# Channel mixer of a decoder layer: gate and up by seven block products over two pairs of chunks, the down projection summed in PSUM in a phase of its own

## The chip, the cores and the metric

The kernel runs on one core of a Trainium2 chip. The metric is the device time of one launch in microseconds (us), median of three runs; the trace is of one more, profiled execution. Engines are called as in the profile: PE (TensorE matmuls), PEld (its weight loads), DVE (VectorE), ACT (ScalarE), POOL (GpSimd), SP (the queue that issues most DMAs).

## The reference, cut to what matters

One layer: a token mixer (RWKV-7, mLSTM, sliding-window and forgetting attention, then an output projection) and a channel mixer. Only the second is changed:

```
D_MODEL, SEQ, D_FF = 1024, 2048, 2816                       # float32
h = _rmsnorm(x, norm_ffn_pre)
gate, up = jnp.split(h @ ffn_w_up, 2, axis=-1)               # 2048x1024 @ 1024x5632
gate = _causal_dwconv(gate, ffn_conv_w, ffn_conv_b)          # width 3, along the sequence
f = jax.nn.gelu(gate, approximate=True) * up
x = x + _rmsnorm(f @ ffn_w_down, norm_ffn_post)              # 2048x2816 @ 2816x1024
```

## The kernel before

Each float32 operand of a large product is scaled by a power of two and split into two float16 parts, high and low. One product of two numbers is then three float16 matmuls: high x high, high x low, low x high. The 2048 tokens are four chunks of 512 (`C`), each four tiles of 128 (`P`); the 2816 channels are 22 blocks of 128 (`NF`).

`stage2` ends with the output projection. `o_tiles(c)` works on the four token tiles of chunk c: load of y, split, two DMA transposes into `yt` (one buffer), 96 matmuls of 128x256, norm, add to x, a second norm (`norm_u`, with two `rsqrt`, each a `pow` on POOL), two DMA transposes into the operand `U2[c]` (`V` in the profile). `o_tiles(2)` and `o_tiles(3)` come last.

`stage_n`, lines 1463 to 1552, is the channel mixer. A loop over 11 groups `g` of two channel blocks loads and splits the group's weights: `split_w` loads pieces of 128x1024 through the stage tile `wst`, takes the maximum on DVE (L233), reduces it over the partitions with `partition_all_reduce` on POOL (L238), makes the power of two by three tiny DVE operations (`pow2`, L204 to L206), writes the high part on ACT (L252) and the low one on DVE (L253). Then for each chunk and block: `gemm_cm` (L265 to L267), 24 matmuls of 128x512 into `psg` for the gate and 24 into `psu` for up; ACT copies the gate to `gb` (L1504), DVE makes the convolution (L1508 to L1510), ACT the GELU (L1511), DVE the product with `psu` (L1515) and its maximum (L1516). After both blocks a `partition_all_reduce` (L1519) gives the scale, ACT and DVE split f (L1526, L1527), and for each token tile and half of the outputs six matmuls (L1535 to L1537) make a partial sum in `psd` that DVE adds to the accumulator `acc` in SBUF (L1541). The last group ends with norm, residual and store (L1543 to L1552). All 16 `acc` tiles live in SBUF.

A planner (the tile framework with a timeline simulation) puts the instructions of each engine in a fixed order; on the chip each engine takes them in that order, so a waiting instruction holds up all behind it on its engine.

Of the kernel before, what the change touches and what calls it, by code (L numbers as in the profile page):

```python
# [97 lines left out]
def _layout(inp):  # L98
# [19 lines left out]
    up = a["ffn_w_up"].reshape(KT, P, 2, NF, P).transpose(3, 1, 0, 2, 4)  # L118
# [21 lines left out]
class Trunk:  # L140
# [14 lines left out]
    def setup(self):  # L155
# [19 lines left out]
        for n, k in enumerate(("g1", "g2")):  # L175
# [6 lines left out]
            nc.vector.tensor_scalar(out=self.ug[:, n:n + 1], in0=un, scalar1=2.0 ** -9, scalar2=None, op0=ALU.mult)  # L182
# [17 lines left out]
    def pow2(self, m, e):  # L200

        nc = self.nc
        o = self.small.tile([P, 3], F32, name="p2")
        nc.vector.tensor_scalar(out=o[:, 0:1], in0=m, scalar1=1e-30, scalar2=2.0 ** -e, op0=ALU.max, op1=ALU.mult)  # L204
        nc.vector.tensor_scalar(out=o[:, 1:2].bitcast(I32), in0=o[:, 0:1].bitcast(I32), scalar1=0x7F800000, scalar2=None, op0=ALU.bitwise_and)
        nc.vector.reciprocal(out=o[:, 2:3], in_=o[:, 1:2])  # L206
        return o[:, 1:2], o[:, 2:3]
# [83 lines left out]
    def norm_u(self, pool, x, n, grow, U, i, h=None, bufs=1):  # L291
# [6 lines left out]
        self.rsqrt(ss[:, 1:2], ss[:, 0:1], 2.0 ** -18 / D, 2.0 ** -18 * EPS)  # L298
# [563 lines left out]
    def stage2(self):  # L862
        with ExitStack() as ck, ExitStack() as co:
# [597 lines left out]


    def stage_n(self):
        nc = self.nc
        GF = 2
        NG = NF // GF
        with ExitStack() as ctx:
            small = self.pool(ctx, "small_n", bufs=4)
            sw = self.pool(ctx, "small_nw", bufs=2)
            self.wp = self.pool(ctx, "w_n", bufs=1)  # L1470
            self.stage = self.pool(ctx, "st_n", bufs=2)
            wk = self.pool(ctx, "wk_n", bufs=2)
# [112 lines left out]
```

## Time and profile before

| | us |
|---|---|
| median of 3 runs | 3137.87 (3135.27 to 3146.45) |
| the profiled execution | 3138.18 |
| its span, first to last instruction | 3136.0 |
| output projection over (last matmul on `Wo`) | about 1753 |
| last matmul of the channel mixer | about 3117.6 |

A row of a group of instructions has the line, the engine, the operation, output <- inputs, shape and count, then busy time, mean ns of one, and the idle time of the engine before it with what ended it. A matmul's row overlaps the next one's, so the pace is read from starts or from counts in a window. Times in a timeline are us from the start of the span.

### The profile page before, as it was taken

The numbers are of one execution on the slowest core, as the hardware profiler recorded it, in microseconds if no ns is written. First come the engines' busy times: TensorE is split into PE (matmuls) and PEld (weight loads), VectorE is DVE, ScalarE is ACT, GpSimd is POOL, SyncE is SP. The second block draws the span as 40 slices with busy tenths as digits, with TensorE's granted clock in tenths as the row PEclk, the third lists the DMA queues.
The fourth block names the chain that finished last, engine by engine and source line by source line (L and its number), as shares of the span: only waits on it lengthen the run. The fifth ranks groups of instructions, "written<-read, shape, count | busy, mean of one in ns | idle before, by whom it ended". The sixth has DMA issues, their size and how long they took to land. (4 is left out here: it accounts for less than half of the span.)

```text
span 3136.0 us, 46311 instructions
## 1 busy us (share of the span) xinstructions
PE 2840.9 (91%) x17902; PEld 1697.3 (54%) x17902; DVE 1893.1 (60%) x4159; ACT 942.1 (30%) x1812; POOL 599.5 (19%) x957
## 2 busy tenths in 40 slices
PE   1599889999989998799987899999999999999995
PEld 0145577777767776577764444444444444444442
DVE  3464565568776554577765565655656656556565
ACT  2342232345452224366652221111211211212121
POOL 1243222223324332132221100000000000000033
PEclk9799899998988999799998899999999999999998
DMA  6442323345652365565544210000100100001023
GB/s 177 101 111 60 91 68 101 88 107 137 153 138 77 86 184 150 142 151 140 125 109 108 61 41 14 27 27 14 41 14 28 41 14 27 28 14 41 14 101 114
DMA packets 322396, 256.08 MB, mean 82 GB/s; under 512 B 215488, under 2 KB 269120, under 8 KB 322176
## 3 DMA queue, kind: packets, MB, share of 16 engines
q1 hardware_dynamic: 252320, 200.67, 23.6%
q10 hardware_dynamic: 69856, 52.46, 6.0%
q8 instruction: 140, 2.29, 0.3%
q14 instruction: 80, 0.66, 0.1%
HBM read 153.26 MB, written 66.49 MB: 70 GB/s over the span
## 5 line engine op out<-in xcount | busy, mean ns | idle before, releaser
L1541 DVE SCALAR_TENSOR_TENSOR acc<-psd,uns,acc 128x512 f32<-128x512 f32 x320 | 237.1, 750 | 209.2 <-PE psd L1537 207.9
L1535 PE MATMUL psd<-hi_dn,fh 128*128 128x512 f16 x704 | 269.8, 383 | 18.2 <-ACT fh L1526 18.1
L267 PE MATMUL psg<-V,lo_up 128*128 128x512 f16 x704 | 268.8, 382 | 9.4 <-DVE lo_up L253 9.4
L1536 PE MATMUL psd<-lo_dn,fh 128*128 128x512 f16 x704 | 269.5, 383 | 0.0
L265 PE MATMUL psg<-V,hi_up 128*128 128x512 f16 x704 | 268.7, 382 | 0.0
L266 PE MATMUL psg<-V,hi_up 128*128 128x512 f16 x704 | 268.7, 382 | 0.0
L267 PE MATMUL psu<-V,lo_up 128*128 128x512 f16 x704 | 267.4, 380 | 0.0
L266 PE MATMUL psu<-V,hi_up 128*128 128x512 f16 x704 | 267.1, 379 | 0.0
L265 PE MATMUL psu<-V,hi_up 128*128 128x512 f16 x704 | 267.1, 379 | 0.0
L1537 PE MATMUL psd<-hi_dn,fl 128*128 128x512 f16 x704 | 262.4, 382 | 1.8 <-DVE fl L1527 1.8
L267 PEld LDWEIGHTS <-lo_up 128*128 128x128 f16 x1408 | 138.1, 98 | 176.4 <-DVE lo_up L253 9.9
L265 PEld LDWEIGHTS <-hi_up 128*128 128x128 f16 x1408 | 138.0, 98 | 166.5 <-issue 1.7
L266 PEld LDWEIGHTS <-hi_up 128*128 128x128 f16 x1408 | 138.0, 98 | 166.5 <-issue 1.4
L275 PE MATMUL psg<-Wo,yt 128*128 128x256 f16 x512 | 144.7, 284 | 42.8 <-DMA yt<-hl 42.7
L1504 ACT ACTIVATE gb<-psg,un_up 128x512 f32<-128x512 f32 x88 | 60.2, 684 | 386.4 <-PE psg L267 386.4
L265 PE MATMUL psg<-U,hi_cm 128*128 128x512 f16 x256 | 103.9, 406 | 69.7 <-ACT hi_cm L252 69.7
L1506 POOL COPY gtail<-gb 128x2 f32<-128x2 f32 x88 | 19.8, 225 | 768.6 <-ACT gb L1504 768.6
L233 DVE TENSOR_REDUCE wm<-wst 128x1 f32<-128x1024 f32 (+1 forms) x91 | 109.7, 1206 | 88.5 <-DMA wst<-in_w_up 50.7
L265 PE MATMUL psf<-U,hi_fm 128*128 128x256 f16 x576 | 162.3, 282 | 0.0
L267 PE MATMUL psf<-U,lo_fm 128*128 128x256 f16 x576 | 162.2, 282 | 0.0
L266 PE MATMUL psf<-U,hi_fm 128*128 128x256 f16 x576 | 162.1, 281 | 0.0
L277 PE MATMUL psg<-Wo,yt 128*128 128x256 f16 x512 | 141.6, 281 | 5.2 <-DMA yt<-hl 5.2
(428 smaller groups left out, 6400.7 us busy)
## 6 DMA issues: line engine op xcount, KB each, us to landing
wst<-in_w_up SPq DMA_DIRECT2D x44, 512.0 KB
wst<-in_w_dn SPq DMA_DIRECT2D x22, 512.0 KB
zin<-zR SPq DMA_DIRECT2D x80, 128.0 KB
ka<-kA ACTq DMA_DIRECT2D x40, 256.0 KB
wst<-in_w_cm SPq DMA_DIRECT2D x17, 512.0 KB
zR<-m SPq DMA_DIRECT2D x32, 256.0 KB
wso<-in_w_o SPq DMA_DIRECT2D x32, 256.0 KB
xr<-in_x ACTq DMA_DIRECT2D x16, 512.0 KB
```

The costliest lines, as they stand in the source:

```text
L233: nc.vector.tensor_reduce(out=m[:, i:i + 1], in_=st[:, :w], axis=AX.X, op=ALU.max, apply_absolute_value=True)
L265: nc.tensor.matmul(ps[:, sl], lhsT=hi[:, k, n0:n0 + nn], rhs=uh[:, k, sl], start=k == 0, stop=False)
L266: nc.tensor.matmul(ps[:, sl], lhsT=hi[:, k, n0:n0 + nn], rhs=ul[:, k, sl], start=False, stop=False)
L267: nc.tensor.matmul(ps[:, sl], lhsT=lo[:, k, n0:n0 + nn], rhs=uh[:, k, sl], start=False, stop=k == KT - 1)
L275: nc.tensor.matmul(ps, lhsT=uh[:, k, sl], rhs=hi[:, k, n0:n0 + nn], start=k == 0, stop=False)
L277: nc.tensor.matmul(ps, lhsT=ul[:, k, sl], rhs=hi[:, k, n0:n0 + nn], start=False, stop=k == KT - 1)
L1504: nc.scalar.activation(out=gb[:, 2:], in_=pg, func=AF.Copy, scale=un)
L1506: nc.gpsimd.tensor_copy(out=prev[jj], in_=gb[:, C:C + 2])
L1535: nc.tensor.matmul(ps, lhsT=fh[:, jj, sl], rhs=dh[:, o], start=jj == 0, stop=False)
L1536: nc.tensor.matmul(ps, lhsT=fh[:, jj, sl], rhs=dl[:, o], start=False, stop=False)
L1537: nc.tensor.matmul(ps, lhsT=fl[:, jj, sl], rhs=dh[:, o], start=False, stop=jj == GF - 1)
L1541: nc.vector.scalar_tensor_tensor(out=acc[t][:, ns], in0=ps, scalar=uns, in1=acc[t][:, ns], op0=ALU.mult, op1=ALU.add)
```

## The change

The channel mixer becomes two phases.

First phase. The chunks form two pairs. For one channel block and one pair, gate and up of both chunks are a 2x2 block product: weights (gate, up) x (lower, upper half of the 1024 inputs) times activations (halves of the inputs) x (two chunks). It is made by seven block products instead of eight, with three sums of weight blocks (`S`) and four of activations (`T`, made once per pair by `combine`). The products are accumulated in part in three PSUM tiles a, b, c (two buffers each): a product is added to a bank that ACT or DVE has read before. The 22 blocks are taken one at a time; `up_weights` loads and prepares the next block's weights, forms `S` with four POOL operations and takes the maximum of the down weights; `ffn_up` makes the products, the convolution, GELU and product over both chunks at once, stores f as float32 to DRAM (`fD`) and notes its maximum. `f_scale` makes one scale per chunk at the end.

Second phase. `ffn_down` loads the down weights again (split once, kept in SBUF) and f from DRAM, splits f and sums all 22 blocks in PSUM: for chunk 0 in eight banks with the block as the outer loop, for chunks 1 to 3 tile by tile. Then scale, norm, residual and store. The accumulator in SBUF is gone.

The diff, cut to its core (the layout of `w_up`, the vector form of `pow2` and two scale exponents are left out):

```diff
@@ stage2
                     if c <= 2:
                         self.o_tiles(c - 1)
             ck.close()
-            u2b = self.pool(self.ctx, "u2b")
+            keep = self.pool(self.ctx, "keep_n")
...
+            u2b = self.pool(self.cb, "u2b")
             for c in range(2, NC):
                 self.U2[c] = u2b.tile([P, 2, KT, C], F16, name=f"V{c}")
+            self.Tc = [u2b.tile([P, 4, 2, 4, C], F16, name="T0")]
+            self.tails = {}
             for c in range(2, NC):
                 self.o_tiles(c)
+                if c == 2:
+                    self.combine(0, lambda n: self.ow.tile([P, 4, W], F32, name="xs"), self.Tc[0])
+    def combine(self, p, buf, T):
...
+        for k in range(4):
+            for t in range(0, C, W):
...
+                for n, o in enumerate((0, 2, 1, 3)):
+                    nc.gpsimd.tensor_tensor(out=x[:, o], in0=B[n][:, 0, k, ts], in1=B[n][:, 1, k, ts], op=ALU.add)
+                for o, a, b in ((0, 1, 0), (1, 3, 1), (3, 3, 0), (2, 2, 3)):
+                    nc.vector.tensor_tensor(out=x[:, o], in0=x[:, a], in1=x[:, b], op=ALU.subtract)
+                nc.scalar.copy(out=T[:, :, 0, k, ts], in_=x)
+                nc.vector.tensor_tensor(out=T[:, :, 1, k, ts], in0=x, in1=T[:, :, 0, k, ts], op=ALU.subtract)
@@ stage_n
+            W = {j: self.up_weights(j) for j in range(2)}
...
+            for j in range(2):
+                self.ffn_up(0, j, W[j])
+            self.combine(1, ...)
+            for j in range(2):
+                self.ffn_up(1, j, W.pop(j))
+            for j in range(2, NF):
...
+                if j + 1 < NF:
+                    W[j + 1] = self.up_weights(j + 1)
+                w = W.pop(j)
+                for p in range(2):
+                    self.ffn_up(p, j, w)
+                    if j == NF - 1:
+                        self.f_scale(p)
...
+        self.ffn_down()
+    def up_weights(self, j):
+        W = self.wp.tile([P, 2, 7, C], F16, name="Wup")             # two buffers
+        R = self.raw.tile([P, 4, C], F32, name="raw", tag="raw")    # one buffer
+        nc.sync.dma_start(out=R.rearrange("p s n -> p (s n)"), in_=self.A["w_up"][j])
...
+        nc.vector.tensor_reduce(out=m[:, 0:1], in_=R..., op=ALU.max, apply_absolute_value=True)
+        nc.gpsimd.partition_all_reduce(m[:, 1:2], m[:, 0:1], P, RMAX)
+        un, sc = self.pow2(m[:, 1:2], 12)
+        nc.vector.tensor_tensor(out=m[:, 2:3], in0=un, in1=self.ug[:, 1:2], op=ALU.mult)
+        S = self.raw.tile([P, 3, C], F32, name="S")
+        gt = lambda o, x, y, op: nc.gpsimd.tensor_tensor(out=o, in0=x, in1=y, op=op)
+        gt(S[:, 1], R[:, 2], R[:, 0], ALU.subtract)
+        gt(R[:, 0], R[:, 0], R[:, 1], ALU.add)
+        gt(S[:, 0], R[:, 0], R[:, 2], ALU.subtract)
+        gt(S[:, 2], R[:, 3], S[:, 0], ALU.subtract)
+        for o, x in ((slice(0, 4), R), (slice(4, 7), S)):
+            nc.scalar.activation(out=W[:, 0, o], in_=x, func=AF.Copy, scale=sc)
+            nc.vector.scalar_tensor_tensor(out=W[:, 1, o], in0=x, scalar=sc, in1=W[:, 0, o], ...)
+        nc.sync.dma_start(out=d, in_=self.A["w_dn"][j])
+        nc.vector.tensor_reduce(out=self.mD[:, j:j + 1], in_=d, ...)
+    def ffn_up(self, p, j, w):
...
+        product(a, 2, "B11", True)          # 12 matmuls of 128x512 each
+        nc.scalar.activation(out=X, in_=a, func=AF.Copy, scale=un)
+        product(b, 4, "T2", True)
+        add(g2, b, X)                       # DVE: out = b * un + X
+        product(a, 3, "B21", False)         # added to what stands in a
+        nc.scalar.activation(out=gb[:, 2:C + 2], in_=a, func=AF.Copy, scale=un)
+        product(b, 5, "T3", False)
+        add(up[:, 1], b, X)
+        product(c, 0, "T1", True)
+        add(up[:, 1], c, up[:, 1])
+        product(b, 1, "T4", False)
+        add(up[:, 0], b, X)
+        product(c, 6, "B22", False)
+        add(g2, c, g2)
...
+        nc.scalar.activation(out=t, in_=gb[:, 2:], func=AF.Identity, scale=fw(2), bias=...)      # 128x1024
+        nc.vector.scalar_tensor_tensor(out=t, in0=gb[:, 1:2 * C + 1], scalar=fw(1), in1=t, ...)
+        nc.vector.scalar_tensor_tensor(out=t, in0=gb[:, 0:2 * C], scalar=fw(0), in1=t, ...)
+        nc.scalar.activation(out=t, in_=t, func=AF.Gelu_apprx_tanh)
+        nc.gpsimd.tensor_tensor(out=t, in0=t, in1=up..., op=ALU.mult)
+        nc.sync.dma_start(out=self.fD[j][:, p * 2 * C:(p + 1) * 2 * C], in_=t)
+        nc.vector.tensor_reduce(out=self.mF[:, 2 * p:2 * p + 2, j:j + 1], in_=F, ...)
+    def ffn_down(self):
...
+            for j in range(NF):
+                weights(j)                  # ACT queue: load 512 KB (three buffers); ACT high part, DVE low part
+                f = values(0, j)            # SP queue: load 256 KB (four buffers); ACT high part, DVE low part
+                for i in range(NSUB):
+                    for n in range(2):
+                        mms(ps[i][n], f, i, n, j)               # 3 matmuls of 128x512
+                    if j == NF - 1:
+                        out(0, i, ps[i])
+            for c in range(1, NC):
+                F = [values(c, j) for j in range(NF)]           # 30 buffers for f in all
+                for i in range(NSUB):
+                    ps = [bank() for n in range(2)]
+                    for j in range(NF):
+                        for n in range(2):
+                            mms(ps[n], F[j], i, n, j)
+                    out(c, i, ps)
```

## Rows read from the trace of the kernel before

**Rows 1.** The page: the line of PE's busy share, the granted clock in 40 slices of the span, and what the DMA engines moved in each.

```profile
PE 2840.9 (91%) x17902; PEld 1697.3 (54%) x17902; DVE 1893.1 (60%) x4159; ACT 942.1 (30%) x1812; POOL 599.5 (19%) x957
...
PEclk9799899998988999799998899999999999999998
...
GB/s 177 101 111 60 91 68 101 88 107 137 153 138 77 86 184 150 142 151 140 125 109 108 61 41 14 27 27 14 41 14 28 41 14 27 28 14 41 14 101 114
```

**Rows 2.** Busy time of each engine by stretch of the span: end of the output projection, the channel mixer up to its last chunk, 200 us of its middle, and three stretches at the end. Columns: from:to, length, busy us (and count) of PE, PEld, DVE, ACT, POOL, granted clock, DMA share, GB/s.

```profile
1633.60:1753.10 119.50, 81.72 (x525) 54.16 (x524) 58.51 (x99) 35.79 (x57) 20.80 (x23) 0.83 0.44 115
1753.10:3092.80 1339.70, 1331.18 (x6147) 599.84 (x6144) 807.46 (x1347) 245.97 (x340) 108.36 (x265) 1.00 0.10 33
2000.00:2200.00 200.00, 200.00 (x928) 90.24 (x926) 117.25 (x199) 33.05 (x46) 9.41 (x35) 1.00 0.06 19
3092.80:3104.00 11.20, 0.00 (x0) 0.00 (x0) 4.46 (x9) 1.29 (x3) 1.42 (x2) 0.62 0.51 161
3104.00:3117.60 13.60, 13.21 (x48) 5.24 (x48) 7.49 (x13) 4.13 (x8) 2.34 (x3) 0.81 0.00 0
3117.60:3136.00 18.40, 0.00 (x0) 0.00 (x0) 6.53 (x7) 1.15 (x2) 10.09 (x6) 0.64 0.46 171
```

**Rows 3.** The first stretch of rows 2 again, only the matmuls that read the operand V of the channel mixer: length, PE busy and count, clock, DMA share, GB/s.

```profile
1633.60:1753.10 119.50, 35.77 (x141) 0.83 0.44 115
```

**Rows 4.** Groups of DVE instructions by line, between 2000 and 2400 us (busy, mean ns, idle before).

```profile
L1541 DVE SCALAR_TENSOR_TENSOR acc<-psd,uns,acc 128x512 f32<-128x512 f32 x104 | 77.0, 750 | 66.3 <-PE psd L1537 66.0
L233 DVE TENSOR_REDUCE wm<-wst 128x1 f32<-128x1024 f32 x20 | 24.4, 1220 | 25.9 <-DMA wst<-in_w_up 16.7 <-DMA wst<-in_w_dn 9.2
...
L1510 DVE SCALAR_TENSOR_TENSOR gc<-gb,pc,gc 128x512 f32<-128x512 f32 x26 | 19.5, 751 | 0.6
...
L253 DVE SCALAR_TENSOR_TENSOR lo_up<-wst,p,hi_up 128x1024 f16<-128x1024 f32 x12 | 15.1, 1280 | 1.5 <-ACT hi_up L252 1.5
```

**Rows 5.** The same view and stretch for ACT.

```profile
L1504 ACT ACTIVATE gb<-psg,un_up 128x512 f32<-128x512 f32 x25 | 17.1, 685 | 128.8 <-PE psg L267 128.8
...
L252 ACT ACTIVATE hi_up<-wst,p 128x1024 f16<-128x1024 f32 x12 | 13.1, 1141 | 35.4 <-PE psu L266 35.1
```

**Rows 6.** The same view for POOL, the whole span.

```profile
L1551 POOL TENSOR_TENSOR wst<-wst,acc 128x1024 f32<-128x1024 f32 x16 | 39.5, 2471 | 18.2 <-DMA wst<-x2buf 7.8 <-DVE acc L1550 6.5 <-DVE rsq L214 4.0
L427 POOL TENSOR_TENSOR m<-z 128x512 f32<-128x512 f32 x32 | 35.2, 1100 | 22.0 <-issue 22.0
```

**Rows 7.** POOL's timeline in the token mixer and the output projection: start, length, line, operation; in brackets the idle time before and what ended it ("issue": nothing that the profile shows).

```profile
88.93 1.03 POOL L427 TENSOR_TENSOR m<-z 128x512 f32<-128x512 f32 x1 [7.19 <-issue]
...
102.56 0.38 POOL L238 PARTITION_ALL_REDUCE wmm<-wm  x1 [5.90 <-issue]
...
380.69 0.71 POOL L534 TENSOR_TENSOR bon<-bon,r_ln_b 128x256 f32<-128x256 f32 x1 [7.08 <-issue]
...
1674.00 0.38 POOL L238 PARTITION_ALL_REDUCE wmm<-wm  x1 [11.72 <-DVE rsq L214]
```

**Rows 8.** DVE's timeline at two of those places.

```profile
90.00 0.75 DVE L428 SCALAR_TENSOR_TENSOR m<-m,pc,z 128x512 f32<-128x512 f32 x1 [7.04 <-POOL m L427]
90.66 0.15 DVE L205 TENSOR_SCALAR p<-p 128x1 int32<-128x1 int32 x1
...
1650.55 0.15 DVE L204 TENSOR_SCALAR p<-wmm 128x1 f32<-128x1 f32 x1 [6.19 <-POOL wmm L238]
1650.62 0.74 DVE L1509 SCALAR_TENSOR_TENSOR gc<-gb,pc,gc 128x512 f32<-128x512 f32 x1
```

**Rows 9.** PE's timeline behind the second of them.

```profile
1655.07 0.38 PE L266 MATMUL psg<-V,hi_up 128*128 128x512 f16 x1
1664.85 0.61 PE L267 MATMUL psg<-V,lo_up 128*128 128x512 f16 x1 [9.41 <-DVE lo_up L253]
1665.25 0.64 PE L265 MATMUL psg<-V,hi_up 128*128 128x512 f16 x1
1665.68 0.63 PE L266 MATMUL psg<-V,hi_up 128*128 128x512 f16 x1
```

**Rows 10.** The timeline of DVE and POOL near the end: two DVE operations, each beside a POOL operation of 128x1024.

```profile
3091.50 2.34 POOL L1551 TENSOR_TENSOR wst<-wst,acc 128x1024 f32<-128x1024 f32 x1
3091.53 2.86 DVE L1509 SCALAR_TENSOR_TENSOR gc<-gb,pc,gc 128x512 f32<-128x512 f32 x1
...
3120.76 0.73 DVE L1541 SCALAR_TENSOR_TENSOR acc<-psd,uns,acc 128x512 f32<-128x512 f32 x1
3120.85 2.34 POOL L1551 TENSOR_TENSOR wst<-wst,acc 128x1024 f32<-128x1024 f32 x1 [1.16 <-DVE rsq L214]
```

**Rows 11.** The output projection's timeline: the last matmul of one token tile and the first of the next that waited, the transposes between them, and the transposes of the very last tile into V.

```profile
1632.80 0.27 PE L277 MATMUL psg<-Wo,yt 128*128 128x256 f16 x1
1641.13 0.28 PE L277 MATMUL psg<-Wo,yt 128*128 128x256 f16 x1 [0.81 <-DMA yt<-hl]
```

**Rows 12.** SP's DMA issues there.

```profile
1748.40 18.93 SPq L289 DMA_TRANSPOSE V<-hl  x4
```

**Rows 13.** The end of the timeline: the restart of PE after its idle stretch, the last square and the last stores.

```profile
3104.12 0.61 PE L1535 MATMUL psd<-hi_dn,fh 128*128 128x512 f16 x1 [11.41 <-ACT fh L1526]
...
3121.61 1.06 ACT L1548 ACTIVATE njunk<-acc 128x1024 bf16<-128x1024 f32 x1 [4.62 <-DVE acc L1541]
...
3130.21 2.63 SPq L1552 DMA_DIRECT2D out<-wst  x2
```

More of the change, by code (lines that the diff above doesn't have):

```diff
@@ L202, in pow2 @@
         nc = self.nc
[L203 to L207, printed above, removed]
+        n = m.shape[-1]
+        o = self.small.tile([P, 3 * n], F32, name=f"p2_{n}")
+        nc.vector.tensor_scalar(out=o[:, 0:n], in0=m, scalar1=1e-30, scalar2=2.0 ** -e, op0=ALU.max, op1=ALU.mult)
+        nc.vector.tensor_scalar(out=o[:, n:2 * n].bitcast(I32), in0=o[:, 0:n].bitcast(I32), scalar1=0x7F800000, scalar2=None, op0=ALU.bitwise_and)
+        nc.vector.reciprocal(out=o[:, 2 * n:3 * n], in_=o[:, n:2 * n])
+        return o[:, n:2 * n], o[:, 2 * n:3 * n]
     def rsqrt(self, out, v, mul, eps):
@@ new lines, in stage_n @@
+            self.sn = self.small = self.pool(ctx, "small_n", bufs=4)
+            self.raw = self.pool(ctx, "raw_n", bufs=1)
+            self.wp = self.pool(ctx, "w_n", bufs=2)
+            self.wk = self.pool(ctx, "wk_n", bufs=2)
+            self.psw = self.pool(ctx, "ps_w", bufs=2, space=PSUM)
+            tp = self.pool(ctx, "t1_n", side="right")
+            W = {j: self.up_weights(j) for j in range(2)}
+            self.Tc.append(tp.tile([P, 4, 2, 4, C], F16, name="T1"))
+            for j in range(2):
+                self.ffn_up(0, j, W[j])
@@ new lines, in f_scale @@
+    def f_scale(self, p):
+        nc, small = self.nc, self.sn
+        self.small = small
+        if p == 0:
+            md = small.tile([P, 2], F32, name="md", bufs=1)
+            nc.vector.tensor_reduce(out=md[:, 0:1], in_=self.mD, axis=AX.X, op=ALU.max)
+            nc.gpsimd.partition_all_reduce(md[:, 1:2], md[:, 0:1], P, RMAX)
+            un, sc = self.pow2(md[:, 1:2], 14)
+            nc.vector.tensor_copy(out=self.sd[:, 0:1], in_=un)
+            nc.vector.tensor_copy(out=self.sd[:, 1:2], in_=sc)
+        mm = small.tile([P, 4], F32, name="mm")
+        nc.vector.tensor_reduce(out=mm[:, 0:2], in_=self.mF[:, 2 * p:2 * p + 2], axis=AX.X, op=ALU.max)
+        nc.gpsimd.partition_all_reduce(mm[:, 2:4], mm[:, 0:2], P, RMAX)
+        un, sc = self.pow2(mm[:, 2:4], 14)
+        nc.vector.tensor_scalar(out=self.sf[:, 2 * p:2 * p + 2, 0], in0=un, scalar1=self.sd[:, 0:1], scalar2=None, op0=ALU.mult)
+        nc.vector.tensor_copy(out=self.sf[:, 2 * p:2 * p + 2, 1], in_=sc)
@@ L1554, in run @@
     def run(self):
-        self.cu, self.cr_, self.cf = ExitStack(), ExitStack(), ExitStack()
+        self.cu, self.cr_, self.cf, self.c2, self.cb = (ExitStack() for n in range(5))
         self.setup()
@@ L1561, in run @@
         if "N" in self.phases:
-            if "2" not in self.phases:
-                self.u2p = self.pool(self.ctx, "u2")
-                self.U2 = [self.u2p.tile([P, 2, KT, C], F16, name=f"V{c}") for c in range(NC)]
-                for c in range(NC):
-                    self.nc.sync.dma_start(out=self.U2[c], in_=self.pre_u[c])
             self.stage_n()
```

196 lines of the change are left out of this document (106 added, 90 removed).

## The prediction

> **What bounds the kernel now.** I read the page first: PE is busy 91% of the span, with the clock at its upper level in the second half [rows 1]. A busy share is no rate, so the windows come next. In the middle of the channel mixer PE starts 928 matmuls of 128x512 in 200 us, one every 0.2155 us, without a gap, while DVE is busy 59% and DMA idle [rows 2]. So this stage is bound by the number of matmuls. From 1753.1 to 3092.8 us stand 6147 of them; at that pace they take 1324.7 of 1339.7 us, so 15.0 are lost. Behind come 11.2 us without PE (the last chunk's scale), 48 matmuls in 13.6 us instead of 10.3, and a tail of 18.4 us [rows 2]. The reader should see a front end too: before 1753.1 the mixer had already run 141 matmuls in holes of the output projection [rows 3], worth 30.4 us. So the mixer stands as if it had begun at 1722.7 and run without filler: 1413.3 us = 6336 x 0.2155 (1365.4) + 47.9 lost.
>
> **The change, part by part.**
>
> Matmuls. Gate and up took 22 blocks x 4 chunks x 48 = 4224; seven products of 12 for 2 pairs make 22 x 2 x 84 = 3696. The down projection keeps 22 x 4 x 4 x 2 x 3 = 2112. So 528 fewer, 113.8 us at the pace of [rows 2]: 3696 take 796.5 us (36.2 per block), 2112 take 455.1.
>
> Removed beside PE: 320 additions into acc, 750 ns each [rows 4], about 240 us of DVE, and the scales per chunk. They stood beside matmuls and are worth nothing by themselves.
>
> Load per block in the first phase, by the durations of [rows 4 to 6]. DVE: ten additions out of PSUM 7.5 us, four convolution steps of 128x1024 at 1.28, maxima of f 2.4, of the weights 2.4 and 1.2, low parts of 128x2048 and 128x1536 by the slope from 0.75 (512) to 1.28 (1024) 2.3 + 1.8, small ones 0.6: 23.3 of 36.2 us, or 64%, against 59% now. ACT: four evacuations 2.7, and some 8 for the wide operations at 1.14 for 1024 columns: 30%. POOL: two products 4.9, four sums at 1.1, an all-reduce 0.4: 9.7. No engine but PE is full; the matmul bound stays, if the waits allow.
>
> The waits are the point. In-place accumulation makes PE wait for an engine inside a unit (one block, one pair): a's second product needs ACT's read of the first, and three products on b and c need DVE's read of what stands there. Each read is due while one other product runs, 12 x 0.2155 = 2.59 us; result latency, read (0.75) and signal take some 1.1, so DVE may be 1.5 us late and no more. Queued behind a DVE instruction that waits are just these reads, and behind them PE.
>
> And DVE will wait, for POOL. On POOL each change between the all-reduce and a TENSOR_TENSOR costs a pause that no instruction explains: 5.90 us into the reduce, 7.08 and 7.19 back out of it; one reduce whose pause fell into waiting time started at once [rows 7], so the pause counts from POOL's previous instruction. The planner doesn't foresee it: DVE stood 7.04 us at a waiting operation with a ready one (L205) behind it, and 6.19 us in the same way at L204 [rows 8], after which PE idled 9.41 us [rows 9]. In the middle of the mixer now POOL runs only reduces and copies, so it never changes. The new phase changes twice per block. Placed as the program has it: subtraction (1.1), all-reduce, three sums (3.3). The reduce is due about 2.6 us after the weights land and comes at 1.1 + 5.9 = 7.0: DVE's `pow2` stands B = 4.4 us. POOL then is through 17.8 us after landing (7.0 + 0.4 + 7.1 + 3.3), while the product of a unit falls due at about 12: it is 5.8 us late, less what PE lost before, and DVE stands some 4.3 us again at the maximum of f. Of a stand of B, 1.5 us are slack and DVE's spare 36% of the mean way to the next urgent read (3.9 us, from their distances 5.2, 2.6 and 10.3) returns 1.4. So PE loses 1.5 us the first time, and about 1.0 the second, when POOL has partly caught up: 2.5 per block, 55 us in all. Bounds: 0, if the reduces fall into POOL's idle time, and both pauses less slack, (5.9 - 1.5) + (7.1 - 1.5) = 10.0 per block, 220 us. I take 55 as each way in part is covered by POOL's spare 26 us per block.
>
> The port. A DVE operation with two SBUF inputs took 2.86 us beside a POOL operation of 2.34, one that reads PSUM and SBUF its usual 0.73 [rows 10]. The Trainium skill (SBUF — State Buffer, Who interferes with whom) says the same: only two SBUF inputs, or the two-port modes, contend with GpSimd. By it the new reads out of PSUM stay free, and six two-input operations per block meet 9.3 us of POOL work that was not there; taking the rows' delays for an estimate, 1 to 2 us of DVE per block, inside the slack. Without the rule, by the rows alone, the sum is the same: nothing added, at most 22 x 1.4 = 31 us.
>
> The front. The last four token tiles took 119.5 us [rows 2]. Without matmuls of the mixer between them the chain is 96 matmuls of 256 columns, at half of 0.2155 each 10.3 us, plus 8.3 from the last one to the next tile's [rows 11], about 19 to 20: over at 1633.6 + 78 = 1712. The first pair's `combine` (32 POOL sums, 24 us of DVE) and two all-reduces with four pauses stand on the same queues: I put the end at 1730, between 1712 and 1753. The first unit's work tiles probably share memory with the projection's (40 KB of weights and 28 of work tiles beside some 170 of operands and new pools, by the shapes in the code), free when the last transposes land, 1767.3 [rows 12], 14 us after the last matmul. Three of seven products (7.8 us) fit ahead of that: 7 lost (0 to 14). The second `combine` starts then too, takes some 40 us of DVE beside the units' own work and is covered by two units (36.2): 10 lost (0 to 25). So the mixer stands as if begun at 1747 instead of 1722.7: 24 us worse, between 11 better and 70 worse.
>
> The turn between phases. f of chunk 0 needs the first pair's scale, whose chain runs beside the last unit (18.1 us); first weights and values can be split before. 5 us, between 0 and 20 (today's like gap took 11.2 [rows 13]).
>
> The second phase. Chunk 0 takes in 768 KB per block of 5.17 us, 152 GB/s, and the next chunk's values beside it; the profile shows 171 GB/s at a DMA share of 0.46 [rows 2] and 184 in a slice [rows 1]. 5 us, between 0 and 25. Chunks 1 to 3 need a 256 KB value per 1.29 us only for a quarter of their time, with 30 buffers: 2. The DRAM round trip writes 1 MB per block in the first phase beside 1.5 MB of loads: 69 GB/s, hidden. Tail: last sum, square 1.06 and its chain, one store [rows 13]: 10.5 us by adding 0.9, 1.3, 0.3, 0.8, 1.4, 1.3 and some 4.5 for the store.
>
> Sum: 1747 + 3696 and 2112 matmuls 1251.6 + 55 + 5 + 5 + 2 + 10.5 = 3076 for the span. The profiled run took 2.2 more than its span (3138.18), and stands 0.3 above the median: 3078, 60 us or 1.9% faster.
>
> **The rivals.**
>
> A. The pauses are hidden: POOL idles 26 us of 36.2 per block. Then 55 us less: 3023.
>
> B. POOL holds up DVE in full, place: `pow2` behind the reduce and the maximum of f behind the product. 220 instead of 55: 3243. It speaks for it that [rows 8, 9] show just this, and that reads are more urgent here. It decides the sign where a block loses over (3138 - 3023) / 22 = 5.2 us.
>
> C. The clock. Lost time of 1 to 3 us comes in every unit. Rows: after 9.41 us of idling, matmuls start 0.425 us apart, the lower level, 1.2 GHz [rows 9]; in the dense middle the granted clock is 1.00 [rows 2]. If a fifth of the first phase falls to the lower level, 0.2 x 796.5 = 159 more: 3237. The Trainium skill (TensorE: Matmul & The Clock Gate, A second HAM failure mode: psum-queue depth-cycling) warns of this: PE pausing briefly between groups of matmuls as banks are cycled can swing the clock between its levels. No row here shows it for pauses under 5 us.
>
> D. The change doesn't give a second phase that PE bounds: chunk 0 is fed at the 101 GB/s of an early slice [rows 1]. 22 x 0.786 MB take 171 us instead of 114: 3135, no change.
>
> **How the numbers follow.** A measurement of this kernel can tell some 0.5%, 16 us, from no change. My forecast 3078 with its own range 3040 to 3125: 0.55, of which 0.50 is faster and 0.05 same. A: 0.17, faster. B: 0.18, of which 0.15 is slower and 0.03 same, since a partial loss between forecast and B is as likely as B itself. C: 0.05, slower. D: 0.05, same. Together 0.67 faster, 0.13 same, 0.20 slower. The range goes from a little under A, 3015, to 3180, the half of B that lies next to the forecast; what is left out is a front end at its best with A, and the rest of B and C.
>
> **What would show it.** Right: 36 to 41 us per block in the first phase, DVE idle before `pow2` and before the maximum of f with POOL as releaser, POOL pauses of 6 to 7 us twice per block, granted clock near 1.00. A: windows with a start every 0.2155 us. B: PE idle over 5 us per block, released by DVE. C: a granted clock under 0.95 from 1770 to 2600. The front: the last matmul on `Wo` near 1730. The turn: PE idle under 10 us where `fD` is first read. Wrong altogether if a queue that I counted as hidden (ACT behind its DMA issues, SP behind the store of f) shows up as PE's releaser.

## The result and the profile after

The changed kernel takes 3190.69 us (median; 3186.59 to 3195.55), the kernel before on the same chip 3142.16: a ratio of 1.0146, 95% interval 1.0099 to 1.0193. It is 1.5% slower; forecast was 1.9% faster, and 3190.69 lies above the range's 3180. The profiled run took 3187.6, its span is 3185.6 us, 109.6 over the 3076 of the sum. Matmul counts are as forecast. One run of e12_sums_vector below took 8700.25 us; its median and ratio go by the other three.

The page of the changed kernel, the lines that answer to [rows 1]: busy time, granted clock by slice, GB/s by slice.

```profile
PE 2780.7 (87%) x17374; PEld 1665.5 (52%) x17374; DVE 1707.7 (54%) x3515; ACT 1043.6 (33%) x1844; POOL 808.4 (25%) x990
PEclk9799889899989998899987789999999999999999
GB/s 177 102 109 58 92 66 104 91 95 147 150 134 65 109 167 167 128 139 133 122 90 126 94 125 53 53 53 44 54 49 53 53 53 40 290 107 87 66 73 20
```

PE is less busy than before (91%). Its windows by stage, against [rows 2]: length, then busy time and count of PE, PEld, DVE, ACT, POOL, granted clock, DMA share, GB/s. The stages are the first 200 us of the first phase, its rest, the turn, the second phase, the tail.

```profile
1751.20:1951.20 200.00, 148.79 (x604) 62.66 (x605) 125.44 (x139) 46.57 (x43) 60.99 (x64) 0.85 0.29 98
1951.20:2692.30 741.10, 695.57 (x3093) 308.49 (x3091) 386.94 (x423) 190.87 (x182) 192.30 (x178) 0.97 0.13 50
2692.30:2717.80 25.50, 0.00 (x0) 0.10 (x1) 6.80 (x16) 4.17 (x5) 3.07 (x3) 0.57 0.40 132
2717.80:3176.30 458.50, 458.45 (x2112) 207.21 (x2111) 125.05 (x154) 109.80 (x154) 44.66 (x30) 0.99 0.31 105
3176.30:3185.60 9.30, 0.11 (x1) 0.00 (x0) 3.41 (x4) 1.40 (x3) 0.55 (x1) 0.72 0.14 56
```

Read them by the pace of [rows 2], 0.2155 us a matmul. What a stretch takes beyond its count at that pace is called its loss from here on. 604 matmuls are worth 130.2 us: the start loses 69.8. 3093 are worth 666.5: the rest loses 74.6, though its PE looks 94% busy: 45.5 us stand idle (741.10 - 695.57), and the other 29.1 are matmuls slower than the pace. The turn stands 25.5 us without a matmul. The second phase is dense: 458.5 for 455.1.

Where the 74.6 go shows in one block. The timeline of POOL, DVE and PE (start, length, engine, line; in brackets the idle time before and its releaser):

```profile
2150.98 1.27 POOL L1537 TENSOR_TENSOR S<-raw 128x512 f32<-128x512 f32 x1 [16.39 <-DVE up L1568]
2152.21 2.35 POOL L1602 TENSOR_TENSOR F<-F,up 128x1024 f32<-128x1024 f32 x1
2160.82 0.38 POOL L1533 PARTITION_ALL_REDUCE wm<-wm  x1 [6.25 <-issue]
2168.45 1.44 POOL L1537 TENSOR_TENSOR raw<-raw 128x512 f32<-128x512 f32 x1 [7.25 <-issue]
...
2154.59 1.22 DVE L1604 TENSOR_REDUCE mF<-F 128x2 f32<-128x1024 f32 x1 [0.77 <-POOL F L1602]
2161.22 0.15 DVE L205 TENSOR_SCALAR p<-wm 128x1 f32<-128x1 f32 x1 [5.41 <-POOL wm L1533]
...
2161.74 0.74 DVE L1568 SCALAR_TENSOR_TENSOR up<-psb,wm,X 128x512 f32<-128x512 f32 x1
...
2157.19 2.75 PE L1565 MATMUL psc<-V,Wup 128*128 128x512 f16 x12
2162.54 4.44 PE L1565 MATMUL psb<-T,Wup 128*128 128x512 f16 x12 [2.60 <-DVE up L1568]
2166.81 2.75 PE L1565 MATMUL psa<-V,Wup 128*128 128x512 f16 x12
```

POOL ends the product f at 2154.56, pauses 6.25 us without a releaser, runs the all-reduce, pauses 7.25 us again. DVE stands 5.41 us at `pow2` (L205). The addition behind it (L1568, a read that PE waits for) starts at 2161.74, and PE idles 2.60 us. Then twelve matmuls take 4.44 us instead of 2.75: the clock has fallen to its lower level. One block loses 2.6 + 1.7 = 4.3 us.

The waits between 1960 and 2560 us, some 15 blocks (who waited for whom: us in all, times, longest):

```profile
DVE p L205 <- POOL wm L1533: 75.1, 14, 5.7
DVE mF L1604 <- POOL F L1602: 50.9, 29, 4.1
...
PE psb L1565 <- DVE up L1568: 39.1, 15, 2.9
```

So DVE stands 5.4 + 3.5 us a block behind POOL, and PE idles 2.6. These are all the waits of PE in the rest (its groups by form; the three other groups, `psa` and `psc`, have none):

```profile
L1565 PE MATMUL psb<-T,Wup 128*128 128x512 f16 x1332 | 329.5, 401 | 45.5 <-DVE up L1568 45.5
```

The start has one thing more, the reductions for the maximum of the down weights (tile view: count, durations, first and last start; below, what their engine waited for):

```profile
L1548 DVE TENSOR_REDUCE mD<-rd x22: 1203/1210/1220, 1757.7 to 1916.2; 128x1 f32<-128x1024 f32 x22
...
  DMA rd<-in_w_dn: 10.5, 6
```

All 22, meant one a block, were drawn into the first 165 us. They depend on nothing but a load. The last matmul on `Wo` (same view) answers to the 1730 of the forecast:

```profile
L276 PE MATMUL psg<-Wo,yt x512: 272/273/437, 1288.7 to 1736.4; 128*128 128x256 f16 x171
```

The turn, timeline of DVE, ACT with its DMA issues, and PE:

```profile
2697.75 0.16 DVE L1622 COPY sf<-p 128x2 f32<-128x2 f32 x1
...
2712.78 0.17 DVE L1622 COPY sf<-p 128x2 f32<-128x2 f32 x1
...
2713.03 1.31 ACTq L1638 DMA_DIRECT2D wdr<-in_w_dn  x3
...
2714.87 0.72 ACT L1649 ACTIVATE f<-fr,sf 128x512 f16<-128x512 f32 x1 [11.90 <-issue]
2716.65 1.15 ACT L1642 ACTIVATE Wd<-wdr,sd 128x1024 f16<-128x1024 f32 x1 [1.05 <-DMA wdr<-in_w_dn]
...
2717.85 42.43 PE L1656 MATMUL psd<-Wd,f 128*128 128x512 f16 x184 [25.59 <-ACT Wd L1642]
```

Chunk 0's scale is there at 2697.75. Its weights are asked for at 2713.03, after the second pair's scale.

### The profile page after: what moved, and what is told of

Same layout as the page of the kernel before. It is cut to its first block, busy times and chain, and to the rows that moved or that the text cites. A ratio compares the mean times of both kernels' runs of the same rounds, so it can differ in the third digit from the quotient of the medians.

```text
span 3185.6 us, 45085 instructions
## 1 busy us (share of the span) xinstructions
PE 2780.7 (87%) x17374; PEld 1665.5 (52%) x17374; DVE 1707.7 (54%) x3515; ACT 1043.6 (33%) x1844; POOL 808.4 (25%) x990
## 4 chain that ended last, share of the span: by engine, by line
PE 44%; issue 11%; DVE 10%; DMA 9%; POOL 4%; ACT 3%; SPq 0%; ACTq 0%; POOLq 0%; DVEq 0%
PE psd L1656 10%; PE psb L1565 6%; PE psc L1565 3%; PE psa L1565 3%; DMA raw<-in_w_up 3%; DVE Wup L1544 2%; POOL F L1602 2%; PE psf L268 1%; PE pso L1338 1%; PE psf L266 1%; PE psf L267 1%; DMA yt<-hl 1%; DMA y<-ybuf 1%; PE psf L276 1%; PE psf L278 1%
## 5 line engine op out<-in xcount | busy, mean ns | idle before, releaser
L1565 PEld LDWEIGHTS <-Wup 128*128 128x128 f16 x3696 | 371.2, 100 | 584.0 <-issue 148.2
L1656 PE MATMUL psd<-Wd,f 128*128 128x512 f16 x2112 | 458.6, 380 | 25.6 <-ACT Wd L1642 25.6
L1565 PE MATMUL psb<-T,Wup 128*128 128x512 f16 x1584 | 400.3, 406 | 84.9 <-DVE up L1568 64.2
L1656 PEld LDWEIGHTS <-f 128*128 128x128 f16 x2112 | 207.3, 98 | 276.8 <-ACT f L1649 23.9
L1565 PE MATMUL psa<-V,Wup 128*128 128x512 f16 x1056 | 252.1, 385 | 25.0 <-ACT Wup L1543 21.8
L276 PE MATMUL psg<-Wo,yt 128*128 128x256 f16 x512 | 148.4, 290 | 49.8 <-DMA yt<-hl 41.6
L278 PE MATMUL psg<-Wo,yt 128*128 128x256 f16 x512 | 144.5, 287 | 6.2 <-DMA yt<-hl 6.2
L277 PE MATMUL psg<-Wo,yt 128*128 128x256 f16 x512 | 148.1, 290 | 0.0
L276 PE MATMUL psf<-hi_fv,U 128*128 128x256 f16 (+1 forms) x512 | 139.1, 278 | 2.0 <-ACT zc L779 2.0
L277 PE MATMUL psf<-lo_fv,U 128*128 128x256 f16 (+1 forms) x512 | 139.1, 277 | 0.0
L278 PE MATMUL psf<-hi_fv,U 128*128 128x256 f16 (+1 forms) x512 | 139.0, 277 | 0.0
L268 PE MATMUL psg<-U,lo_cm 128*128 128x512 f16 x256 | 103.2, 404 | 33.1 <-DVE lo_cm L254 19.0
L1328 ACT ACTIVATE fP<-psf,ln2k 128x512 f32<-128x512 f32 (+3 forms) x160 | 98.2, 624 | 98.6 <-PE psf L1324 41.8
L1568 DVE SCALAR_TENSOR_TENSOR up<-psb,wm,X 128x512 f32<-128x512 f32 x88 | 65.8, 747 | 110.5 <-PE psb L1565 110.3
```

The costliest lines, as they stand in the source:

```text
L268: nc.tensor.matmul(ps[:, sl], lhsT=lo[:, k, n0:n0 + nn], rhs=uh[:, k, sl], start=False, stop=k == KT - 1)
L276: nc.tensor.matmul(ps, lhsT=uh[:, k, sl], rhs=hi[:, k, n0:n0 + nn], start=k == 0, stop=False)
L277: nc.tensor.matmul(ps, lhsT=uh[:, k, sl], rhs=lo[:, k, n0:n0 + nn], start=False, stop=False)
L278: nc.tensor.matmul(ps, lhsT=ul[:, k, sl], rhs=hi[:, k, n0:n0 + nn], start=False, stop=k == KT - 1)
L1328: nc.scalar.activation(out=e[:, o:], in_=ps[:, o:], func=AF.Exp, scale=-1.0, bias=self.ln2k)
L1565: nc.tensor.matmul(ps, lhsT=W[:, a, n, ks], rhs=rhs[u](b, k), start=first and k == 0 and i == 0, stop=k == 3 and i == 2, skip_group_check= ...
```

## The experiments

Theory: GpSimd's pauses around the all-reduce make VectorE, which works in order, stand at `pow2` and at the maximum of f; PE waits for the reads queued behind it, and its clock adds to that. Rivals: VectorE is too slow for the folds; the port that GpSimd shares with it; the two phases as such. Times are medians, ratios against the kernel before on the same chip. All stage lengths are of single profiled executions. The runs stand on two chips, and a difference of a few us between two of them says nothing by itself. The code ahead of the mixer is the same in most runs and yet ends its attention anywhere from 1620 to 1658 us, so stages are compared by length and loss, not by place.

**Who makes PE wait**

```diff
 # e1_vector_sums
-gt = lambda o, x, y, op: nc.gpsimd.tensor_tensor(...)
+gt = lambda o, x, y, op: nc.vector.tensor_tensor(...)
-nc.gpsimd.tensor_tensor(out=t, in0=t, in1=up, op=mult)
+nc.vector.tensor_tensor(out=t, in0=t, in1=up, op=mult)
```

> The four weight sums of a block and its two products f go from GpSimd to VectorE, so that GpSimd keeps the all-reduces, the small copies and the memsets and no longer pauses between two kinds of programs inside a block. Theory (VectorE stands in order behind the all-reduce, 5.4 us a block, because GpSimd pauses 6 to 7 us on each side of it; TensorE loses 2.6 us of waiting a block and 1.7 us more at the lower clock after it): the 74.5 us lost between 1950 and 2692 us fall under 25, the time falls by 45 to 75 us. Rival (VectorE itself is too slow a reader of the products): VectorE gets 4 x 0.75 + 2 x 1.28 = 5.6 us more work a block, the loss grows, and the time rises by 20 to 100 us.

3068.12 us, ratio 0.9749 (0.9716 to 0.9782): 123 us under the changed kernel. Windows of its first phase, first 200 us and rest:

```profile
1759.60:1959.60 200.00, 177.30 (x768) 77.07 (x769) 161.43 (x188) 57.08 (x53) 30.02 (x45) 0.94 0.31 109
1959.60:2593.90 634.30, 632.59 (x2930) 286.40 (x2928) 439.74 (x506) 180.34 (x172) 20.13 (x70) 1.00 0.15 55
```

2930 x 0.2155 = 631.4 of 634.3: a loss of 2.9 instead of 74.6, with VectorE busy 69% instead of 52%. The start loses 34.5 instead of 69.8, the turn 17.0 instead of 25.5; I had counted on the rest alone, so the time fell by more than I expected. VectorE is not too slow.

```diff
 # e2_no_reduce
-nc.gpsimd.partition_all_reduce(m[:, 1:2], m[:, 0:1], P, RMAX)
+nc.vector.tensor_copy(out=m[:, 1:2], in_=m[:, 0:1])
```

> The all-reduce of each weight block's maximum is left out: every partition uses its own maximum (one copy on VectorE), so the powers of two differ between partitions. The sums and the products stay on GpSimd. Theory (pauses around the all-reduce, and VectorE's wait behind it): the loss between 1950 and 2692 us falls from 74.5 to under 20, the time by 50 to 75 us. Rival (the port: GpSimd's sums and products slow VectorE and hold it off): they all remain, and the time stays within 15 us.

3076.68 us, ratio 0.9782 (0.9746 to 0.9817): 114 us under the changed kernel. The same windows, and two groups of VectorE in the second:

```profile
1737.70:1937.70 200.00, 174.75 (x758) 75.96 (x759) 148.70 (x164) 55.62 (x52) 71.40 (x67) 0.92 0.31 108
1937.70:2573.60 635.90, 634.64 (x2939) 287.39 (x2937) 382.85 (x419) 181.34 (x173) 172.86 (x153) 1.00 0.15 55
```
```profile
L1568 DVE SCALAR_TENSOR_TENSOR up<-psb,wm,X 128x512 f32<-128x512 f32 x72 | 53.9, 749 | 144.1 <-PE psb L1565 143.4
...
L1535 DVE TENSOR_TENSOR wm<-p,ug 128x1 f32<-128x1 f32 x16 | 15.5, 971 | 0.0
```

Sums and products stay on GpSimd, 172.86 us of busy time with its small copies, and the loss is 2.5; the start loses 36.6 instead of 69.8. GpSimd's work beside VectorE costs PE nothing here, so the port falls; what costs is the change of programs. The Trainium skill's rule (SBUF — State Buffer, Who interferes with whom), that only two SBUF inputs or the two-port modes contend with GpSimd, agrees: the additions out of PSUM take their 749 ns, and a tiny product of two SBUF inputs (L1535), beside GpSimd's sums here, takes 971 ns instead of the 140 of the changed kernel.

```diff
 # e4_product_vector: only the product
-nc.gpsimd.tensor_tensor(out=t, in0=t, in1=up, op=mult)
+nc.vector.tensor_tensor(out=t, in0=t, in1=up, op=mult)
```

> Only the product f goes to VectorE; the weight sums stay on GpSimd, so a block still has one change from sums to all-reduce and one back. Theory (the pause belongs to each change between the two kinds of programs, and VectorE stands behind the all-reduce): most of it stays, the loss from 1950 us to the end of the first phase is over 45 us and the time is 0 to 30 us under the changed kernel's 3190. Rival (the waits of the maximum of f for GpSimd's product, 77 us in 37 waits, are the cause): the loss falls under 25, the time by 50 to 75 us.

3119.29 us, ratio 0.9915 (0.9884 to 0.9946): 71 us better, as the rival said: the start gives 16 (it loses 53.9), the rest 50. Its seven runs spread from 3107.56 to 3140.77, and the profiled one is the slowest. Windows, two of its waits between 1960 and 2560, and PE's timeline in a block:

```profile
1780.00:1980.00 200.00, 161.78 (x678) 69.12 (x679) 138.48 (x156) 50.07 (x47) 53.19 (x62) 0.89 0.29 101
1980.00:2655.30 675.30, 654.43 (x3020) 295.14 (x3018) 434.27 (x455) 187.32 (x178) 126.80 (x138) 1.00 0.14 54
```
```profile
DVE p L205 <- POOL wm L1533: 57.4, 16, 4.0
...
PE psb L1565 <- DVE up L1568: 20.0, 16, 1.6
```
```profile
2159.84 2.75 PE L1565 MATMUL psb<-T,Wup 128*128 128x512 f16 x12 [1.18 <-DVE up L1568]
```

My expectation was wrong: both pauses stay, the loss falls to 24.5. The maximum of f no longer waits for POOL, and the stand at `pow2` shrinks from 5.4 to 3.6 us, as the pause before the all-reduce now counts from the sum, not from the product after it; how much each of the two gives is not separated here. PE idles 1.25 us a block, and behind 1.18 us of idling twelve matmuls take their 2.75: the clock stays up.

```diff
 # e12_sums_vector: only the sums
-gt = lambda o, x, y, op: nc.gpsimd.tensor_tensor(...)
+gt = lambda o, x, y, op: nc.vector.tensor_tensor(...)
```

> Only the four weight sums of a block go to VectorE; the product f stays on GpSimd, just ahead of the all-reduce as before. Theory (the pause before the all-reduce is counted from the last other GpSimd instruction, and that is the product; so the all-reduce's result comes no earlier): the stand at the power of two stays near 5.4 us a block and the loss after the first 200 us over 55, the time 3170 to 3195 less what the start gives. Rival (GpSimd's amount of work counts, the sums being 5 of its 10 us a block): the loss halves or better, the time falls by over 40 us.

3191.18 us, ratio 1.0134 (1.0090 to 1.0178): no gain, though GpSimd does half the work. The start loses 49.6 instead of 69.8, but the loss after the first 200 us grows to 99.8 (746.1 - 2999 x 0.2155). Its waits between 1950 and 2560:

```profile
DVE mF L1604 <- POOL F L1602: 92.9, 15, 7.6
...
DVE p L205 <- POOL wm L1533: 51.9, 14, 4.1
```

The stand at `pow2` is 3.7 us, less than I had written, but the maximum of f now stands 6.2: the scheduler has put one of a block's two products behind the all-reduce and its second pause.

```diff
 # e11_late: pow2 and the split of block j+1 after pair 0 of block j
-W[j + 1] = self.up_weights(j + 1)          # load, all-reduce, pow2, sums, split
+n = self.up_weights(j + 1)                 # load, all-reduce, sums
 self.ffn_up(0, j, w)
+m[:, 1:2] += 0 * g2[:, 0:1]                # g2: the last fold of the pair
+W[j + 1] = self.up_split(j + 1, n)         # pow2, split
```

> The changed kernel with one thing moved: VectorE takes the all-reduce's result of the next block only after the last fold of the first pair, half a block later (one 128x1 instruction more a block ties it there); sums, product and all-reduce stay on GpSimd, with their pauses. Theory (what costs is VectorE standing in order at the power of two, not the pauses as such): the loss after the first 200 us of the mixer, 74.6 us, falls under 25, the time by 45 to 75 us from 3190. Rival (GpSimd's pauses themselves, by delaying the product f and so the maximum of f on VectorE): the stand moves to the maximum of f, and the loss stays over 50.

3238.08 us, ratio 1.0294 (1.0261 to 1.0327), the slowest. The theory as I had put it here falls, its rival is right. Waits between 1950 and 2560:

```profile
DVE mF L1614 <- POOL F L1612: 158.9, 14, 12.5
...
PE psb L1574 <- DVE up L1577: 61.8, 14, 5.6
```

VectorE no longer stands at `pow2` at all, but 11.3 us a block at the maximum of f, behind a product that waits for both pauses. The loss after the first 200 us is 122.9. Both rise together over four kernels: VectorE stands 3.6, 8.9, 9.9 and 11.3 us a block (e4, the changed kernel, e12, e11), and a block, 168 matmuls, loses 1.4, 4.1, 5.6 and 6.7.

**The two phases alone**

```diff
 # e5_plain: per pair and block
-product(a, 2, "B11"); product(b, 4, "T2"); ...   # seven, folds on VectorE
+gate c = W2*B1c + W3*B2c; up c = W0*B1c + W1*B2c  # eight, ScalarE evicts
-self.combine(0, ...); self.combine(1, ...); the sums S
```

> The two phases stay, the block products go: gate and up are made by eight plain products (4224 matmuls instead of 3696), without both combines, the three weight sums a block and the folds on VectorE; ScalarE evicts the four results of a pair. Theory (the loss is in what came with the seven products: combines, sums, folds in order behind the all-reduce): the first phase takes 4224 x 0.2155 = 910 us and at most 20 more, it begins at 1735 to 1745 us, and with the turn of 25.6, the second phase of 458 and the tail of 9.5 the time is 3140 to 3165 us, 25 to 50 less than with the seven products. Rival (the loss belongs to the two phases as such: the all-reduce and the product f beside dense matmuls): 4 us a block stay, 22 x 4 = 88, and the time is over 3210 us.

3114.23 us, ratio 0.9886 (0.9856 to 0.9916): faster than before, and 76 us under the seven products as built. Windows from 1753 us, and VectorE's waits in the second:

```profile
1753.00:1953.00 200.00, 192.35 (x881) 86.56 (x880) 74.64 (x72) 54.51 (x61) 32.90 (x31) 0.97 0.22 74
1953.00:2637.00 684.00, 683.79 (x3169) 309.76 (x3166) 202.86 (x196) 191.34 (x216) 90.58 (x96) 1.00 0.13 50
```
```profile
DVE mF L1581 <- POOL F L1579: 171.9, 18, 10.1
...
DVE p L205 <- POOL wm L1528: 76.3, 14, 5.6
```

The all-reduce, its pauses and the product on GpSimd are all still there, VectorE stands behind them longer than in the changed kernel (there 62.0 and 91.0 us in the rest), and yet 3169 matmuls lose 1.1 us. So VectorE's stands cost next to nothing by themselves; they cost where PE waits for VectorE's reads. Here ScalarE reads PSUM, not VectorE, and nothing is accumulated onto a bank that is still being read. It beat my numbers, it seems, because its mixer starts at 1645, in holes of the output projection, and its turn is 11.7 us instead of 25.5. So the two phases gain; the seven products, as built, were what lost.

**The start and the turn**

```diff
 # e3_no_downmax
-load rd <- w_dn[j]; nc.vector.tensor_reduce(out=self.mD[:, j:j+1], in_=rd, op=max)
+nc.gpsimd.memset(self.mD[:, j:j+1], 0.125)
 # e7_combine_vector, in combine
-nc.gpsimd.tensor_tensor(out=x[:, o], in0=hi, in1=lo, op=add)
+nc.vector.tensor_tensor(out=x[:, o], in0=hi, in1=lo, op=add)
```

> The 22 loads of the down weights for their maximum and the 22 reductions (1.21 us each, all drawn between 1757 and 1916 us, six of them waiting 10.5 us for their loads) are left out; the maximum is a constant 0.125. Theory of the start (the 70 us lost before 1950 us are VectorE's queue: 22 x 1.21 = 27 us of reductions, 10.5 us of waits for their loads, the second combine): the time falls by 15 to 38 us. Rival (the second combine with GpSimd's pauses sets the pace of the start, and the reductions only fill its gaps): the time stays within 8 us.

3171.75 us, ratio 1.0084 (1.0052 to 1.0116): 19 better, though the interval overlaps the changed kernel's a little; the first 200 us lose 45.9 instead of 69.8, the rest still 70.9.

> The 64 hi+lo additions of both combines go from GpSimd to VectorE; sums, products and all-reduces stay on GpSimd. Theory (the start is slow because the second combine's additions stand on GpSimd behind the pauses around the all-reduces, 8.8 us in one wait, and VectorE stands behind them): the 70 us lost before 1950 us fall to 40 to 60, the time falls by 8 to 30 us. Rival (VectorE is the full engine of the start, 124 of 199 us, and of the attention): 32 x 0.41 = 13 us more on it in each place, and the time rises by 0 to 25 us.

3172.10 us, ratio 1.0073 (1.0046 to 1.0100): 19 better, too. The first 200 us lose 54.8, the rest 76.8. Times and losses fit both theories. With the 35 of e1 the parts add up to more than the 69.8, so they overlap; that each pushes the others on VectorE is likely, but not shown.

```diff
 # e6_turn
-st = pool("st_d", bufs=4)                    # raw down weights and values
+st = pool("st_d", bufs=4, side="right")      # over the first chunks' activations
-small_n inside the first phase's pools
+small_n kept to the end
```

> The buffers of the second phase's loads are put where the first two chunks' activations lay, which are free from about 2675 us, and the small tiles get memory of their own that is not used again; nothing else changes. Theory (the first down weights were asked for only at 2713 us, behind the last scale, because their buffers lay on memory that was free only then): the 25.6 us without a matmul at the turn become 5 to 12, the time falls by 13 to 20 us. Rival (the turn is the last block's fold, its maximum and the all-reduce, which stay in order on VectorE and GpSimd): the turn stays over 20 us and the time within 5.

3193.04 us, ratio 1.0138 (1.0109 to 1.0167): nothing. The loads are asked for 31 us earlier, from 2681.6 on, and the turn is 21.1 instead of 25.5. A new wait has taken the place of the old one. The next run shows it better.

```diff
 # e8_all: e1 + e6, and
-rd = self.wk.tile(..., tag="rd")             # loads for the maximum: one buffer
+rd = self.raw.tile(..., tag="S")             # the buffer of the sums: one a block
```

> Sums and products on VectorE, the buffers of the second phase on early freed memory, and the loads of the down weights for their maximum through the buffer of the weight sums, so that there is one a block instead of 22 at the start. Theory: against the run with the sums and products on VectorE alone (3068 us; 34 us lost in its first 200 us of the mixer, 17 at the turn) the turn gives 5 to 10 and the start 5 to 20: 3038 to 3058 us, faster than both kernels. Rival (a reduction a block, behind its load, holds VectorE up in the steady blocks): 22 x 1 to 3 us come back and the time is over 3065.

3062.42 us, ratio 0.9722 (0.9703 to 0.9742), 6 under e1 by the medians (the intervals don't tell the two apart) and less than expected: the start loses 25.9, the turn is 18.7. Timeline at the turn, DVE, ACT and PE:

```profile
2569.95 0.17 DVE L1623 COPY sf<-p 128x2 f32<-128x2 f32 x1
...
2587.23 1.15 ACT L1643 ACTIVATE Wd<-wdr,sd 128x1024 f16<-128x1024 f32 x1 [3.26 <-DMA wdr<-in_w_dn]
...
2588.28 1.93 ACT L1650 ACTIVATE f<-fr,sf 128x512 f16<-128x512 f32 x3
...
2589.04 7.25 PE L1657 MATMUL psd<-Wd,f 128*128 128x512 f16 x22 [18.73 <-ACT f L1650]
```

The scale is there at 2569.95, before the last product ends. The first f comes at 2588.28: eight conversions of weights, which wait for their loads, stand ahead of it in ScalarE's order. Its memory was the last block's, free late; the next edit moves that.

```diff
 # e9_early_f: e8, and
-f = fp.tile(..., bufs=NF + 8)
+f = f0.tile(..., bufs=4) if c == 0 and j < 4 else fp.tile(..., bufs=NF + 4)   # f0: side="right"
```

> The run with all three edits, and the first four scaled blocks of f of chunk 0 in memory of their own where the first chunks' activations lay, so that ScalarE's order has them ahead of the fourth weight conversion instead of behind the eighth. Theory (at the turn the scale of chunk 0 is there at the last product, and TensorE waits 18.7 us because the first f, whose memory was the last block's, stood in ScalarE's order behind eight conversions and their loads): the turn falls from 18.7 to 4 to 9 us, the time from 3062 to 3046 to 3054. Rival (the loads hold it: three buffers of weights, each back in over 3 us): TensorE starts early but waits between blocks for 10 us and more, and the time stays within 5 of 3062.

3049.55 us, ratio 0.9685 (0.9650 to 0.9720). PE's timeline at the turn:

```profile
2577.69 2.75 PE L1566 MATMUL psc<-V,Wup 128*128 128x512 f16 x12
2581.07 0.39 PE L1658 MATMUL psd<-Wd,f 128*128 128x512 f16 x1 [0.63 <-ACT f L1651]
2582.47 20.66 PE L1658 MATMUL psd<-Wd,f 128*128 128x512 f16 x95 [1.02 <-DVE Wd L1645]
```

The turn is 0.63 us and three more waits of about 1. The time fell by 13, 12 by the ratios, as the theory had it.

> The same, and the 64 hi+lo additions of the combines on VectorE. Theory (as in the changed kernel, where it gave 18 us): the mixer begins 5 to 10 us earlier and the 26 us lost in its first 200 us fall by 5 to 12, the time is 8 to 20 us under the run without it. Rival (without GpSimd's sums there is no pause left for the additions to stand behind, and VectorE, 150 of the first 200 us, is the full engine): the time is the same within 5 us, or up to 15 longer.

The edit is e7's, on e9. 3034.61 us, ratio 0.9638 (0.9606 to 0.9670), the best: 3.6% under the kernel before, 5.0% under the changed one by the two ratios. Windows of the start and the rest:

```profile
1755.50:1955.50 200.00, 192.89 (x872) 86.03 (x873) 162.55 (x216) 60.91 (x57) 7.63 (x22) 0.97 0.20 73
1955.50:2566.30 610.80, 609.89 (x2826) 276.22 (x2823) 441.22 (x503) 179.16 (x171) 19.71 (x67) 1.00 0.20 74
```

The start loses 12.1 us (e9: 27.0), the rest 1.8, with VectorE busy 81% of the start.

## Why the prediction was wrong

The sum against the changed kernel's profile: the first phase's end was forecast at 1747 + 796.5 + 55 = 2598.5 and came at 2692.3 (+93.8); the turn 5, measured 25.5 (+20.5); the second phase 462.1, measured 458.5 (-3.6); the tail 10.5, measured 9.3 (-1.2). That is the 109.6.

- *Matmuls, 113.8 us fewer*: right. With the waits gone (e1) 3696 matmuls run at the pace of [rows 2], and the second phase does in the changed kernel itself.
- *The pauses, 55 us (bounds 0 and 220)*: the right mechanism, shown by e1 and e2, but the term was sized too small. The idle time came as forecast, 45.5 us in the rest or 2.5 a block, and a block took 40.3 us, inside the 36 to 41 that were to show it. That is luck in part: the 2.5 were to be 1.5 behind `pow2` and 1.0 behind the maximum of f, and PE waited once a block, behind `pow2`, which stood 5.4 us instead of 4.4, as the product f came between the sum and the all-reduce. What the term left out is the clock: slower matmuls cost the other 29.1 us, so 4.1 a block and 74.6 in the rest instead of 46. In the start they cost 18.6 more (148.79 - 130.2). I had the clock as rival C, apart from the pauses and for a fifth of the stage, on the ground that no row showed it under 5 us. Here rows do, and so the Trainium skill's warning (TensorE: Matmul & The Clock Gate, A second HAM failure mode: psum-queue depth-cycling) holds in part: the granted clock is 0.97 over the rest and 0.85 in the start, not the lower level for long stretches.
- *The front, "as if begun at 1747"*: the step that failed most. The last matmul on `Wo` at 1736.4 (forecast 1730) is near, in part by luck: attention's last matmul starts at 1630.2 instead of the 1611.5 of the kernel before, and the way from there took 106 us, 12 less than the forecast has; why is not shown. The first matmul of the mixer comes 15 us later, at 1751.2, where the forecast loses 7, and it waits for the conversion of the first weights on ScalarE (14.33 us, L1543). But the second `combine`, "covered by two units: 10 lost (0 to 25)", met all else in the same 200 us, which lose 69.8 where the forecast has 19 (those 10, and 9 of the 55 for pauses): the 22 reductions for the down weights, which I had counted one a block (e3: 24 of it), its additions on GpSimd behind the pauses (e7: 15), sums and product there (e1: 35). So of the 93.8 us some 14 lie before the first matmul and 51 in the start; the clock behind the pauses of the rest is the other 29.
- *The turn, 5 us (0 to 20)*: wrong. "First weights and values can be split before" took no account of where their tiles lie. The first loads' buffers and the first f lay on memory that the last block used, and e6 to e9 show that both had to move before the turn fell to 0.6.
- *The port, nothing; the second phase, 7; the tail, 10.5*: right within 4 us. Rival D (feeding) didn't come: the slice at the turn moved 290 GB/s.
- *Rival B*: what happened is between the forecast and B, plus a little of C. Its point of decision, 5.2 us a block, was not reached by the pauses (4.1); start and turn made up the rest.

Not settled: how the start's 70 us divide, since its three causes overlap, and why attention ends later than in the kernel before.

## What to carry to other kernels

An engine that works in order hands on every stand to whoever waits for the instructions behind it: before moving work to an idle GpSimd, ask which reads of PSUM are queued behind the instruction that will wait for its result. Where the same engine's programs alternate, moving one wait later (e11) or halving the work (e12) moves the stand; taking one kind of program off the engine (e1, e2) removes it. And cost a turn between phases by the memory of its first tiles, not by when their data is there.

## What the runs showed of the hardware

PE's granted clock fell to the lower level after only 2.6 us of idling behind dense matmuls (twelve in 4.44 us instead of 2.75), and stayed up after 1.18 us (2.75). The length of the idling alone does not decide: in the changed kernel one block idled 2.46 us and fell (4.44), another 2.42 us and stayed up, and in e12 one stayed up behind 3.21 us (2.75). What decides is not shown.

```profile
2243.75 2.75 PE L1565 MATMUL psb<-T,Wup 128*128 128x512 f16 x12 [2.42 <-DVE up L1568]
```

GpSimd's pause into the all-reduce counts from the instruction before it: 6.25 us behind the product here, 5.87 us behind the sum where the product was gone (e4), and 5.87 us behind a COPY of 128x2 in e5, where the last TENSOR_TENSOR had ended 14.3 us earlier. VectorE took the four sums and two products of a block, some 5.2 us (4 x 0.68 + 2 x 1.22 in e1), and was up to 72% busy with a loss of 1.8 us (e10).
